# A two-layer decoder in float32 on one core: choosing when ordinary matmul units are put between Strassen units, and regrouping fifteen weight tiles

## The chip, the cores and the metric

The kernel runs on one core of one Trainium2 chip. The metric is the device time of one launch in microseconds (us), lower is better. Three timed runs of the kernel before gave 2006.13, 2009.50 and 2009.53 us, so the median is 2009.5 us.

## The reference

Two layers work on 256 tokens of width 2048, all in float32. Each layer is

```
h  = RMSNorm(x);  z = h @ w_in                      # 2048 -> 3584
A  = chunked spatial gating of gelu(z[:, :2048])
B  = windowed attention on the rest of z
x += concat(RMSNorm(A), RMSNorm(B)) @ w_out         # 2048 -> 2048
h2 = RMSNorm(x)
x += (silu(h2 @ w_gate) * (h2 @ w_up)) @ w_down     # 2048 -> 5632 -> 2048
```

Only the last line is touched by the change in the order of its work. The buffers that the change regroups are used by all the matmuls with weights.

## The kernel before, in words

**Tiles.** Weights come from HBM in tiles of 128 partitions x 1024 float32 (512 KB), each holding two 128x512 blocks. The matmuls with weights take the type float32r, and a weight tile is split into a high and a low part: `split2` (line 91) lets ScalarE copy the raw tile into `wh` (line 97, a CAST in the profile) and VectorE subtract that from the raw tile into `wl` (line 98). A product of two split operands is three matmuls (`mm3`, lines 126 to 129: high x high, high x low, low x high). An *ordinary unit* (`unit`, line 131) is one raw tile against both groups of 128 tokens: 12 matmuls of 128x512.

**Rings.** Raw tiles live in 7 buffers, `wh` in 4 and `wl` in 4, 15 tiles of 4 KB a partition together. A buffer comes free when its last reader is done: a raw buffer after the subtraction on VectorE, `wl` after the last line-128 matmul of its unit, `wh` after the last line-129 matmul. The sum `t1` of the Strassen units also takes a raw buffer. Loads are issued by SyncE (queue SP) in order, each as soon as a raw buffer is free.

**The feed-forward part.** Eleven blocks of 512 columns of w_gate and w_up are computed. Blocks 0, 1 and 2 are computed by ordinary units (`gate_up`). Blocks 3 to 10 are computed by `seven` (line 571), a Strassen scheme with seven products in place of eight for the two token groups and the two matrices. Each of its *Strassen units* (`s_unit`) is one tile against one 128-token operand: 6 matmuls. A block has two phases. In phase A there are four rounds; each loads three raw tiles, makes three further sums of tiles on VectorE (`t1`, `t2`, and `b12` in place, lines 595, 598, 601) and runs four Strassen units into the PSUM tiles m0, m1, m3, m2. A DMA on POOL's queue then adds w_gate's fourth tile onto `t2` in place (line 603), to be kept for phase B. After the rounds, one ScalarE copy and four VectorE operations on 128x512 recombine the banks (lines 609 to 616). In phase B four rounds load two raw tiles each and run three Strassen units into n0, n1, n2, and five VectorE operations and two SiLUs finish the block (lines 630 to 635).

**The order.** Two Python generators are interleaved when the program is written. `s_stream` yields after each Strassen unit and after each recombination; `std_stream` yields after each ordinary unit of `gate_up` and `down`. The loop at lines 696 to 703 says how many ordinary units come in between: 0.575 of one per Strassen unit in phase A, 0.23 in phase B and 2 at each recombination, kept in the account `owed`, at most one at a time between two Strassen units. `down` of a block can't begin until that block's activations have been transposed (`act_T`, lines 559 to 565): the stream then yields False and no ordinary unit is written. After the Strassen blocks the rest of the ordinary units follows alone (line 705). An ordinary unit in this part accumulates in the two PSUM tiles `dacc`; the next group of sums can't start before VectorE has taken both out (`xres`, line 683). A list scheduler then orders the instructions of each engine near the written order; in the trace each engine works its own list off in order.

Of the kernel before, what the change touches and what calls it, by code (L numbers as in the profile page):

```python
# [12 lines left out]
F32 = mybir.dt.float32  # L13
# [8 lines left out]
P = 128  # L22
# [13 lines left out]
NB = 512  # L36
# [8 lines left out]
    ("gu", 0), ("down", (0, 3)), ("gu", 1), ("down", (1, 4)), ("down", (5, 6)), ("gu", 2),  # L45
    ("down", (2, 7)), ("down", (8, 9)), ("down", (10,)),
)
SHARE_A = 0.575
SHARE_B = 0.23
TURN = 2  # L50
RL = 512
WARM = 12

# [12 lines left out]
def trunk(ctx, tc, x, xt, w_in, w_out, w_gate, w_up, w_down, sgu_w, sgu_g, consts,  # L66
# [15 lines left out]
        return t.bitcast(F32)  # L82

    def raw_load(src, parts=1):
        raw = wp.tile([P, 2, NB], F32, tag="raw", name="raw", bufs=7)
        n = 2 // parts
        for i in range(parts):
            nc.sync.dma_start(raw[:, i * n : (i + 1) * n, :], src[:, i * n : (i + 1) * n, :])
        return raw

    def split2(raw):
        wh = wp.tile([P, 2, NB], F32R, tag="wh", name="wh", bufs=4)
        wl = wp.tile([P, 2, NB], F32R, tag="wl", name="wl", bufs=4)
        step = 2 if clock[0] > 1 else 1
        for j in range(0, 2, step):
            src = raw[:, j : j + step, :]
            nc.scalar.copy(wh[:, j : j + step, :], src)  # L97
            nc.vector.tensor_tensor(  # L98
                wl[:, j : j + step, :], src, f(wh[:, j : j + step, :]), ALU.subtract
            )  # L100
        return wh, wl

    clock = [0]
    serial = itertools.count()
    pending = []

# [24 lines left out]
    def unit(src, acts, acc, first, last):  # L131
        raw = raw_load(src, 2 if clock[0] < 4 else 1)
        wh, wl = split2(raw)
        for j in range(2):
            act, aj = acts[j]
            for t in range(NTOK):
                ts = slice(t * P, (t + 1) * P)
                mm3(
                    acc[t], act[:, 0, aj, ts], act[:, 1, aj, ts], wh[:, j, :], wl[:, j, :],
                    first and j == 0, last and j == 1,  # L140
                )
        tick()

    def product(srcs, pairs):
# [114 lines left out]
    for lay in range(L):  # L259
# [299 lines left out]
        def act_T(b, c, sg, pairs_f=pairs_f):  # L559
            ps = pm.tile([P, 2, SEQ], F32, tag="sm", name="ps_f")  # L560
            transpose_pair([sg[t][:, 2 * c * P : (2 * c + 2) * P] for t in range(NTOK)], ps)
            pair = tp.tile([P, 2, 2, SEQ], F32R, tag="aT", name="aT")
            nc.scalar.copy(pair[:, 0], ps)
            nc.vector.tensor_tensor(pair[:, 1], ps, f(pair[:, 0]), ALU.subtract)
            pairs_f.setdefault(b, []).append(pair)

        def act_later(b, sg, act_T=act_T):
# [3 lines left out]
        def seven(b, lay=lay, pairs2=pairs2, ext2=ext2, act_later=act_later):  # L571
            bank = [pa.tile([P, NB], F32, tag="acc", name=f"m{i}") for i in range(4)]

            def s_unit(raw, m, i, op, first, last):
                wh, wl = split2(raw)
                for j in range(2):
                    ah, al = (op(2 * i + j, h) for h in range(2))
                    mm3(bank[m], ah, al, wh[:, j, :], wl[:, j, :], first and j == 0, last and j == 1)
                tick(0.5)

            def a_op(k, t):
                return lambda p, h: pairs2[p][:, h, k, t * P : (t + 1) * P]

            def e_op(n):
                return lambda p, h: ext2[p][:, h, n, :]

            kept = []
            for i in range(4):
                b11 = raw_load(w_gate[lay, b, i, 0])
                b12 = raw_load(w_up[lay, b, i, 0])  # L590
                b22 = raw_load(w_up[lay, b, i, 1])
                t1 = wp.tile([P, 2, NB], F32, tag="raw", name="t1", bufs=7)
                t2 = ap.tile([P, 2, NB], F32, tag="spt", name="t2", bufs=4)
                first, last = i == 0, i == 3
                nc.vector.tensor_tensor(t1, b11, b12, ALU.add)
                s_unit(b11, 0, i, a_op(0, 0), first, last)
                yield SHARE_A
                nc.vector.tensor_tensor(t2, t1, b22, ALU.add)
                s_unit(t1, 1, i, e_op(1), first, last)
                yield SHARE_A  # L600
                nc.vector.tensor_tensor(b12, b12, b22, ALU.add)  # L601
                s_unit(t2, 3, i, e_op(2), first, last)
                nc.gpsimd.dma_start(t2, w_gate[lay, b, i, 1], accum_op=ALU.add)  # L603
                yield SHARE_A
                s_unit(b12, 2, i, e_op(0), first, last)
                yield SHARE_A
                kept.append(t2)
            m1 = zp.tile([P, NB], F32, tag="z", name="m1")
            nc.scalar.copy(m1, bank[0])
            u1 = zp.tile([P, NB], F32, tag="z", name="u1")  # L610
            nc.vector.tensor_tensor(u1, bank[3], m1, ALU.add)
            c22 = zp.tile([P, NB], F32, tag="z", name="c22")
            c21 = zp.tile([P, NB], F32, tag="z", name="c21")
            nc.vector.tensor_tensor(c21, bank[2], u1, ALU.add)
            nc.vector.tensor_tensor(c22, bank[1], c21, ALU.add)
            nc.vector.tensor_tensor(u1, bank[1], u1, ALU.add)
            yield "turn"
            bank = [pa.tile([P, NB], F32, tag="acc", name=f"n{i}") for i in range(3)]
            for i in range(4):
                b21 = raw_load(w_gate[lay, b, i, 1])  # L620
                b22 = raw_load(w_up[lay, b, i, 1])
                first, last = i == 0, i == 3
                s_unit(b21, 0, i, a_op(1, 0), first, last)
                yield SHARE_B
                s_unit(kept[i], 1, i, a_op(1, 1), first, last)
                yield SHARE_B
                s_unit(b22, 2, i, e_op(3), first, last)
                yield SHARE_B
            sg = [m1, c21]
            for t, m in ((0, m1), (1, c21)):  # L630
                nc.vector.tensor_tensor(m, bank[t], m, ALU.add)
                nc.scalar.activation(m, m, AF.Silu, scale=rstd2[t])
            nc.vector.tensor_tensor(u1, bank[2], u1, ALU.add)
            for t, c in ((0, u1), (1, c22)):
                nc.vector.scalar_tensor_tensor(sg[t], c, nrstd2[t], sg[t], ALU.mult, ALU.mult)
            act_later(b, sg)
            yield "turn"

        seven_done = [False]

# [13 lines left out]
        def gate_up(b, even=even, act_later=act_later):  # L654
            acc = yield from even(b, w_gate)
            sg = []
            for t in range(NTOK):
                s = zp.tile([P, NB], F32, tag="z", name="sg")
                nc.scalar.activation(s, acc[t], AF.Silu, scale=rstd2[t])
                sg.append(s)  # L660
            acc = yield from even(b, w_up)
            for t in range(NTOK):
                nc.vector.scalar_tensor_tensor(
                    sg[t], acc[t], rstd2[t], sg[t], ALU.mult, ALU.mult
                )
            act_later(b, sg)

        def down(blocks, final, lay=lay, pairs_f=pairs_f, norm_block=norm_block, ss1=ss1, pairs1=pairs1):
            for n in range(ND):
                while any(len(pairs_f.get(b, [])) < 2 for b in blocks):  # L670
                    yield False
                acc = new_acc() if seven_done[0] else new_acc(pd, "dacc")
                for k, b in enumerate(blocks):
                    for c in range(2):
                        pair = pairs_f[b][c]
                        unit(
                            w_down[lay, b, n, c], [(pair, 0), (pair, 1)], acc,
                            k == 0 and c == 0, k == len(blocks) - 1 and c == 1,
                        )
                        yield True  # L680
                for t in range(NTOK):
                    xs = xres[:, t, n * NB : (n + 1) * NB]
                    nc.vector.tensor_tensor(xs, acc[t], xs, ALU.add)  # L683
                    if final and lay == L - 1:
                        nc.sync.dma_start(out[t * P : (t + 1) * P, n * NB : (n + 1) * NB], xs)
                if final and lay < L - 1:
                    norm_block(n, ss1, pairs1, lay + 1, C_G1)
# [6 lines left out]
                    yield from down(what, k == len(STD_ORDER) - 1)  # L694

        other = std_stream()
        owed = 0.0
        for said in s_stream():
            turn = said == "turn"
            owed += TURN if turn else said  # L700
            for k in range(TURN):
                if (turn or (k == 0 and owed >= 1.0)) and next(other, False):
                    owed -= 1.0
        seven_done[0] = True
        for went in other:
            if not went:
# [89 lines left out]
```

## Time and profile before

| what | value |
|---|---|
| timed runs, median | 2009.5 us |
| profiled execution, own time | 2011.28 us |
| its span, first to last instruction | 2009.6 us, so 1.7 us lie around it |
| granted TensorE clock, mean | 0.995 |
| TensorE matmuls | 8942, of which 8064 of 128x512 with weights |
| HBM traffic | 226 GB/s over the span |
| feed-forward parts | 299 to 980 us and 1300 to 1980 us of the span |

TensorE is the engine that sets the time. A matmul of 128x512 is shown as 0.39 us long, but the next one starts 0.227 us after it, so starts are compared here and not ends. VectorE operations on 128x1024 are shown as 1.22 us long and follow each other every 1.14 us; those on 128x512 are shown as 0.69 us and follow each other every 0.60 us.

### The profile page before, as it was taken

How to read it: one execution, taken by the hardware profiler on the slowest of the kernel's cores; microseconds unless marked ns; L12 is line 12 of the kernel's file. 1: busy time of each engine (PE TensorE's matmuls, PEld its weight loads, DVE VectorE, ACT ScalarE, POOL GpSimd, SP SyncE). 2: the span in 40 equal slices, each digit the busy share in tenths (PEclk: the TensorE clock that was granted, in tenths of full speed). 3: DMA queues.
4: the chain of work that ended last, by engine and by line, in shares of the span. 5: the costliest groups of instructions: out<-in, count | busy, mean ns of one | idle time of the engine just before them, and what ended most of it. 6: DMA issues, size and time to landing. Idle time of an engine off the chain costs nothing.

```text
span 2009.6 us, 24839 instructions
## 1 busy us (share of the span) xinstructions
PE 1971.9 (98%) x8942; PEld 1610.9 (80%) x8942; DVE 1664.0 (83%) x1931; ACT 1154.1 (57%) x1441; POOL 120.0 (6%) x129
## 2 busy tenths in 40 slices
PE   9999999999999999999999999999999999999999
PEld 6778887788878887788887788877888788877887
DVE  6767689989899897889866776889898998978896
ACT  6455566655655565555654655666556565555554
POOL 1211001000000000000002110000000000000000
PEclk9999999999999999999999999999999999999999
DMA  8753558787796876868655445487887878868684
GB/s 313 254 160 130 188 165 262 216 275 236 247 275 219 274 237 231 252 211 286 216 189 184 138 147 188 159 273 219 262 242 248 274 218 272 251 222 264 208 275 154
DMA packets 127772, 453.80 MB, mean 226 GB/s; under 512 B 14064, under 2 KB 16240, under 8 KB 127648
## 3 DMA queue, kind: packets, MB, share of 16 engines
q1 hardware_dynamic: 116288, 411.21, 60.1%
q0 software_dynamic: 11360, 41.00, 11.1%
q8 instruction: 70, 1.15, 0.2%
q14 instruction: 54, 0.44, 0.1%
HBM read 450.02 MB, written 4.23 MB: 226 GB/s over the span
## 4 chain that ended last, share of the span: by engine, by line
PE 83%; DVE 11%; issue 2%; DMA 2%; ACT 1%; POOL 1%; SPq 0%; DVEq 0%; POOLq 0%; ACTq 0%
PE dacc L128 11%; PE dacc L129 11%; PE dacc L127 10%; PE acc L128 8%; PE acc L129 8%; PE acc L127 7%; DVE wl L98 5%; PE m L129 4%; PE m L128 4%; PE m L127 4%; PE n L128 4%; PE n L129 4%; PE n L127 4%; DMA raw<-in_w_up_dram 1%; DVE raw L601 1%
## 5 line engine op out<-in xcount | busy, mean ns | idle before, releaser
L97 ACT CAST wh<-raw 128x1024 fp32r<-128x1024 f32 (+1 forms) x706 | 738.5, 1050 | 565.6 <-PE dacc L129 215.5
L98 DVE TENSOR_TENSOR wl<-raw,wh 128x1024 fp32r<-128x1024 f32 (+1 forms) x706 | 854.4, 1219 | 199.0 <-ACT wh L97 183.9
L97 ACT CAST wh<-t 128x1024 fp32r<-128x1024 f32 x192 | 202.3, 1054 | 186.9 <-PE dacc L129 109.7
L128 PE MATMUL dacc<-wl,aT 128*128 128x512 f32 x640 | 251.4, 393 | 8.5 <-DVE wl L98 8.5
L98 DVE TENSOR_TENSOR wl<-t,wh 128x1024 fp32r<-128x1024 f32 x192 | 233.5, 1222 | 21.5 <-ACT wh L97 16.3
L129 PE MATMUL dacc<-wh,aT 128*128 128x512 f32 x640 | 251.0, 392 | 0.0
L127 PE MATMUL dacc<-wh,aT 128*128 128x512 f32 x640 | 249.7, 392 | 0.7 <-DVE xres L683 0.7
L128 PE MATMUL acc<-wl,hT 128*128 128x512 f32 x448 | 177.0, 395 | 7.9 <-DVE wl L98 7.9
L127 PE MATMUL acc<-wh,hT 128*128 128x512 f32 x448 | 181.2, 407 | 0.8 <-ACT wh L97 0.8
L129 PE MATMUL acc<-wh,hT 128*128 128x512 f32 x448 | 177.1, 395 | 0.0
L127 PE MATMUL m<-wh,ext 128*128 128x512 f32 x384 | 153.3, 399 | 3.7 <-ACT wh L97 3.5
L128 PE MATMUL dacc<-wl,hT 128*128 128x512 f32 x384 | 150.5, 392 | 3.3 <-DVE wl L98 3.3
L128 PE MATMUL m<-wl,ext 128*128 128x512 f32 x384 | 150.6, 392 | 0.6 <-DVE wl L98 0.2
L127 PE MATMUL dacc<-wh,hT 128*128 128x512 f32 x384 | 150.7, 392 | 0.1
L129 PE MATMUL dacc<-wh,hT 128*128 128x512 f32 x384 | 150.2, 391 | 0.0
L129 PE MATMUL m<-wh,ext 128*128 128x512 f32 x384 | 150.0, 391 | 0.0
L128 PEld LDWEIGHTS dacc<-wl,aT 128*128 128x128 f32 x640 | 121.0, 189 | 36.1 <-DVE wl L98 11.1
L127 PEld LDWEIGHTS dacc<-wh,aT 128*128 128x128 f32 x640 | 120.8, 189 | 26.8 <-DVE xres L683 1.6
L129 PEld LDWEIGHTS dacc<-wh,aT 128*128 128x128 f32 x640 | 121.0, 189 | 25.0
L603 POOL DMA_DIRECT2D t<-in_w_gate_dram x64 | 54.5, 852 | 1387.2 <-DVE wl L98 754.6
L127 PE MATMUL acc<-wh,aT 128*128 128x512 f32 x320 | 126.9, 397 | 0.0
L129 PE MATMUL acc<-wh,aT 128*128 128x512 f32 x320 | 125.2, 391 | 0.0
(157 smaller groups left out, 3146.4 us busy)
## 6 DMA issues: line engine op xcount, KB each, us to landing
raw<-in_w_up_dram SPq DMA_DIRECT2D x240, 512.0 KB, 4.7
raw<-in_w_gate_dram SPq DMA_DIRECT2D x176, 512.0 KB, 4.7
raw<-in_w_down_dram SPq DMA_DIRECT2D x176, 512.0 KB, 4.6
raw<-in_w_in_dram SPq DMA_DIRECT2D x108, 512.0 KB, 4.3
raw<-in_w_out_dram SPq DMA_DIRECT2D x64, 512.0 KB, 3.3
t<-in_w_gate_dram POOLq DMA_DIRECT2D x64, 512.0 KB, 7.0
bias<-rdram POOLq DMA_DIRECT2D x8, 512.0 KB, 5.2
xr<-in_xt_dram SPq DMA_DIRECT2D x8, 256.0 KB, 5.7
```

The source lines that it names most:

```text
L97: nc.scalar.copy(wh[:, j : j + step, :], src)
L98: nc.vector.tensor_tensor(wl[:, j : j + step, :], src, f(wh[:, j : j + step, :]), ALU.subtract)
L127: nc.tensor.matmul(acc, ah, wh, start=first, stop=False)
L128: nc.tensor.matmul(acc, ah, wl, start=False, stop=False)
L129: nc.tensor.matmul(acc, al, wh, start=False, stop=last)
L601: nc.vector.tensor_tensor(b12, b12, b22, ALU.add)
L603: nc.gpsimd.dma_start(t2, w_gate[lay, b, i, 1], accum_op=ALU.add)
```

## The change

Two edits.

1. The 15 weight tiles are dealt out anew: 6 raw, 5 `wh`, 4 `wl` in place of 7, 4, 4.
2. The fixed shares are replaced by a running count. Each VectorE operation of the feed-forward part adds to `debt` (1.14 for 128x1024, 0.6 for 128x512), each matmul takes away 0.227 x 0.91 = 0.207. After every Strassen unit and recombination, ordinary units are written until the count is no longer above zero, or the stream yields False. The order inside each stream and all arithmetic stay.

```diff
-SHARE_A = 0.575
-SHARE_B = 0.23
-TURN = 2
+VEC = 1.14
+VEC_P = 0.6
+MM = 0.227
+LOAD = 0.91
...
     def raw_load(src, parts=1):
-        raw = wp.tile([P, 2, NB], F32, tag="raw", name="raw", bufs=7)
+        raw = wp.tile([P, 2, NB], F32, tag="raw", name="raw", bufs=6)
...
     def split2(raw):
-        wh = wp.tile([P, 2, NB], F32R, tag="wh", name="wh", bufs=4)
+        wh = wp.tile([P, 2, NB], F32R, tag="wh", name="wh", bufs=5)
         wl = wp.tile([P, 2, NB], F32R, tag="wl", name="wl", bufs=4)
...
+        vec(1)
         return wh, wl
...
+    debt = [0.0]
+
+    def vec(n, cost=VEC):
+        debt[0] += n * cost
+
+    def pe(n):
+        debt[0] -= n * MM * LOAD
...
     def unit(src, acts, acc, first, last):
...
+        pe(12)
         tick()
...
             def s_unit(raw, m, i, op, first, last):
...
+                pe(6)
                 tick(0.5)
...
-                t1 = wp.tile([P, 2, NB], F32, tag="raw", name="t1", bufs=7)
+                t1 = wp.tile([P, 2, NB], F32, tag="raw", name="t1", bufs=6)
...
                 nc.vector.tensor_tensor(t1, b11, b12, ALU.add)
                 s_unit(b11, 0, i, a_op(0, 0), first, last)
-                yield SHARE_A
+                vec(1)
+                yield
...
-            yield "turn"
+            vec(4, VEC_P)
+            yield
...
                 s_unit(b21, 0, i, a_op(1, 0), first, last)
-                yield SHARE_B
+                yield
...
+            vec(5, VEC_P)
             act_later(b, sg)
-            yield "turn"
+            yield
...
         other = std_stream()
-        owed = 0.0
-        for said in s_stream():
-            turn = said == "turn"
-            owed += TURN if turn else said
-            for k in range(TURN):
-                if (turn or (k == 0 and owed >= 1.0)) and next(other, False):
-                    owed -= 1.0
+        debt[0] = 0.0
+        for _ in s_stream():
+            while debt[0] > 0.0 and next(other, False):
+                pass
```

The count is also fed, with 0.6 for each VectorE operation, in `act_T` (one, and two matmuls' worth taken away), at the end of `gate_up` (two) and for each `xres` in `down`.

More of the change, by code (lines that the diff above doesn't have):

```diff
@@ L564, in act_T @@
             nc.vector.tensor_tensor(pair[:, 1], ps, f(pair[:, 0]), ALU.subtract)
+            vec(1, VEC_P)
+            pe(2)
             pairs_f.setdefault(b, []).append(pair)
@@ L596, in seven @@
                 s_unit(b11, 0, i, a_op(0, 0), first, last)
-                yield SHARE_A
+                vec(1)
+                yield
                 nc.vector.tensor_tensor(t2, t1, b22, ALU.add)
                 s_unit(t1, 1, i, e_op(1), first, last)
-                yield SHARE_A
+                vec(1)
+                yield
                 nc.vector.tensor_tensor(b12, b12, b22, ALU.add)
@@ L603, in seven @@
                 nc.gpsimd.dma_start(t2, w_gate[lay, b, i, 1], accum_op=ALU.add)
-                yield SHARE_A
+                vec(1)
+                yield
                 s_unit(b12, 2, i, e_op(0), first, last)
-                yield SHARE_A
+                yield
                 kept.append(t2)
@@ L616, in seven @@
             nc.vector.tensor_tensor(u1, bank[1], u1, ALU.add)
-            yield "turn"
+            vec(4, VEC_P)
+            yield
             bank = [pa.tile([P, NB], F32, tag="acc", name=f"n{i}") for i in range(3)]
@@ L623, in seven @@
                 s_unit(b21, 0, i, a_op(1, 0), first, last)
-                yield SHARE_B
+                yield
                 s_unit(kept[i], 1, i, a_op(1, 1), first, last)
-                yield SHARE_B
+                yield
                 s_unit(b22, 2, i, e_op(3), first, last)
-                yield SHARE_B
+                yield
             sg = [m1, c21]
@@ L635, in seven @@
                 nc.vector.scalar_tensor_tensor(sg[t], c, nrstd2[t], sg[t], ALU.mult, ALU.mult)
+            vec(5, VEC_P)
             act_later(b, sg)
-            yield "turn"
+            yield
         seven_done = [False]
@@ L665, in gate_up @@
                 )
+            vec(NTOK, VEC_P)
             act_later(b, sg)
@@ L683, in down @@
                     nc.vector.tensor_tensor(xs, acc[t], xs, ALU.add)
+                    vec(1, VEC_P)
                     if final and lay == L - 1:
```

## Prediction

> **What bounds the kernel now.** I read the page's busy shares first, then TensorE's waits, then single stretches, then the timeline.
>
> ```profile
> ## 1 busy us (share of the span) xinstructions
> PE 1971.9 (98%) x8942; PEld 1610.9 (80%) x8942; DVE 1664.0 (83%) x1931; ACT 1154.1 (57%) x1441; POOL 120.0 (6%) x129
> ```
>
> TensorE is busy nearly always, and the change adds and removes no instruction that computes. So only TensorE's stalls can be won, or new ones made. TensorE's waits name them:
>
> ```profile
> PE dacc L128 <- DVE wl L98: 11.8, 8, 1.9
> PE acc L128 <- DVE wl L98: 7.9, 5, 2.9
> PE m L127 <- ACT wh L97: 3.5, 6, 0.6
> PE n L127 <- ACT wh L97: 2.3, 2, 1.1
> ```
>
> Columns: total us, times, longest. It is always the split that is late. In the timeline I took every matmul start that came later than the 0.227 us pitch: clusters above 0.4 us sum to 49 us. Of these 3.3 are the warm-up, 1.1 the first loads, 12.3 lie in the attention parts (at 64 us 1.2, 128 us 3.8, 1088 us 3.5, 1128 us 3.9), and 32.8 in the two feed-forward parts. In layer 0 the latter are: first phase A 1.8; where the first, second and third ordinary gate_up end 2.7, 2.5 and 6.0; at 768 us 4.0. Layer 1 repeats them with 15.7 in place of 17.0. So about 45 us, 2.2%, is all that can be won.
>
> ```profile
> 384.00:408.00 24.00, 22.06 (x98) 16.96 (x98) 23.68 (x24) 13.40 (x15) 1.72 (x3) 1.00 0.88 263
> 440.50:468.10 27.60, 27.60 (x126) 22.84 (x125) 24.48 (x24) 18.38 (x19) 0.00 (x0) 1.00 0.61 190
> 468.10:523.30 55.20, 55.20 (x247) 45.48 (x246) 50.01 (x48) 31.85 (x33) 3.40 (x4) 1.00 0.92 284
> 811.00:834.00 23.00, 19.67 (x81) 14.78 (x80) 21.09 (x22) 11.84 (x14) 2.55 (x3) 0.93 0.86 247
> ```
>
> Columns: length, busy us of PE, PEld, DVE, ACT, POOL, granted clock, DMA share, GB/s. Two stretches without stalls (a phase B at 440 us, a phase A at 468 us) stand between two with. At 384 us VectorE is busy 23.7 of 24.0 us: there it is the bound. The reason is in the code: gate_up has ended, `down` waits for transposed activations, so no ordinary unit may be written for six Strassen units, and those cost VectorE more than TensorE.
>
> **Part 1, the count.** Prices: 1.14 us for a full VectorE operation, 0.6 for a half one (pitches of the trace); on TensorE 1.36 us for a Strassen unit, 2.72 for an ordinary one, 0.45 for four transposes. I tallied both programs, as built, phase by phase. Before: phase A 52 to 56 us of TensorE with VectorE at 0.89 to 0.98 of it, phase B 28 to 30 us at 0.79 to 0.87. After: phase A 57 to 62 us at 0.87 to 0.90 (the first and the seventh are 0.98 and 1.01), phase B 19 to 22 us at 0.93 to 1.00 (the seventh 0.79), with its twelve Strassen units in a row. So ordinary units move from B to A, and about six a layer to the tail behind the Strassen blocks, where VectorE has room (0.7). No DMA is added.
>
> The forecast is made of the stalls one by one. From the end of a block's last n2 unit, I add VectorE's list up to a late subtraction, and TensorE's up to the unit that needs it.
>
> - First gate_up, before: 19 full and 9 half operations, 27.1 us; TensorE gets there after 4 ordinary and 9 Strassen units and 16 transposes, 24.9. 2.2 late; the trace lost 2.7, so the tally is 0.5 low.
> - The same, after: 22 full and 8 half, 29.9; TensorE 5 and 10 units and 12 transposes, 28.6. 1.3 late, with the 0.5 it is 1.8.
> - Second, after: at the worst unit 0.1 late; I take 0.3. Before it had the order of the first (2.5 lost).
> - Third, after: the end of gate_up now falls at the end of phase A. VectorE 35 full and 7 half, 44.1; TensorE 9 and 17 units and 8 transposes, 48.5. Not late; I take 0.5 (before 6.0).
> - First phase A: load 0.98 in both; 1.8 stays.
> - New: at the end of the third Strassen block, the list has two `xres` behind five recombining operations. 5.2 us to the next subtraction against 4.08 + 0.23 until TensorE needs it, and the next `dacc` isn't free earlier: 0.8.
>
> **Part 2, the rings.** Before, ScalarE's copy for the fourth unit ahead waits for a `wh` buffer (325 us of ScalarE's waits end with a `dacc` matmul), then come 1.05 us of copy and 1.22 of subtraction. With five, the copy is done early, and the subtraction waits only for `wl`. The lead over TensorE grows by 1.05 us. The stall at 768 us is this ring: copies for three ordinary units had been made at 761.7, 763.0 and 767.1 but stand behind n1 in TensorE's list; n1's copy got its buffer at 769.6, when n0 was done. I count 0.5 there.
>
> The price is the raw ring. Here I add VectorE's work between the operation that frees a buffer and the first that reads the new load. The median in the feed-forward part falls from 10.3 to 8.0 us. Loads land 4.7 us after issue (w_gate, w_up); where a subtraction comes first, 1.15 for the copy are added. Gaps below that sum to 21 us a layer before and 28 after. Measured, TensorE lost little of the 21, since VectorE has room. The other ends: nothing at all; or a landing of 5.8 us, by which 45 becomes 79 us a layer. I take half of the 7, so 3.5 a layer, as landings near the median are the rule. In the attention and projection parts a raw tile lies ready for 13 us, so a buffer less costs nothing; if that cover were gone it would cost one load, 4.7 us.
>
> More PE instructions now signal (the `wl` release): 1892 instead of 1191. In the trace a line-129 matmul that signals is followed after 227.0 ns, one that doesn't after 227.6, so nothing; bounds 0 to 0.
>
> In attention the new rings also reorder VectorE's list. At 128 us the subtraction stands behind 8.3 us of small operations, among them two waits of 1.5 us for POOL; after the change both requests stand together and one wait is covered. At 1088 us a stretch of 6.7 us is cut to 5.3. Between 0 and 9 of the 12.3 us, I take 5, from these 1.5 twice and 1.4 plus what the slow clock adds.
>
> **A rule beside the rows.** After the stalls at 770 and 829 us, starts are 0.427 us apart seven to eight times, and the granted clock of 811 to 834 us is 0.93. About 25 such starts in the feed-forward parts cost 0.2 each, 5 of the 32.8 us, and go with their stalls. The Trainium skill (TensorE: Matmul & The Clock Gate, "HAM oscillation — how this bites in real kernels") has the clock drop only for idle gaps over about 3.4 us. By that rule stalls of 1.3 and 2.1 us would cost only themselves, and the sum would be 5 us higher, 1997; the trace disagrees.
>
> **The sum.** Feed-forward per layer after: 1.8 + 1.8 + 0.3 + 0.5 + 0.5 + 0.8 = 5.7, two layers 11.4 in place of 32.8: -21.4. Raw ring +7. Attention -5. Together -19.4. Against the profiled execution, 2011.28 - 19.4 = 1991.9, say **1992 us**; its 2009.6 span becomes 1990. It stands 1.8 above the median of the timed runs, so against that the gain is 17.5 us, 0.9%. Without the raw price and with 9 in attention: 1981.
>
> **Rivals.**
>
> - *All feed-forward stalls melt* (chance 0.08): the longer lead also takes the 11.4 us that I left, and the raw ring costs nothing. 2011.3 - 32.8 - 5 = 1973.5. For it speaks that no late split of the waits above is over 2.9 us; against it that VectorE is itself full at 384 us.
> - *The count can't reach the stalls* (0.17): while `down` yields False nothing can be placed, and the deeper `wh` ring doesn't help an engine that is full. Then only the rise of VectorE's work over TensorE's in these places counts: 7.7, 7.7 and 8.4 us become 7.1, 7.1 and 6.4. That is 3.2 a layer and 5 in attention: 2000.
> - *Phase B without ordinary units* (0.13): at 1.00 of TensorE's time the lead isn't rebuilt in B, and five recombining operations and a subtraction (4.14 us) meet a lead of four Strassen units less copy and subtraction, 5.44 - 2.27 = 3.2. 0.9 at 14 boundaries: 1992 + 13, about 2005. The stall-free B at 440 us, at 0.83, can't deny it. The Trainium skill (Perfetto Trace Analysis, "Optimization Strategy") says that a kernel whose bound changes over time may gain by interleaving its regimes; leaving B alone goes against that, and no run here shows it yet.
> - *The raw ring becomes the bound* (0.15), the case on the slower side. Place: phase A, where a round's b12 keeps its buffer to the last unit and the next b12 is issued only then. VectorE's spare time in a layer's Strassen part is 614 - 563 = 51 us by the tally. Gaps reach that at a landing of 5.3 us and 79 at 5.8. The excess of 28 a layer goes to TensorE: 56 in place of 32.8, attention -5: 2011 + 23 - 5 = 2029. For it: a quarter of the raw tiles in the feed-forward part are already read within some 2.4 us of landing; against it: VectorE waited only 9.6 us for loads in `t1`.
>
> **From this to the numbers.** The forecast has the rest, 0.47, by its unknown bounds 1981 to 2003. Range 1978 to 2012: it holds the forecast, the second and the third rival, 0.77, and the first steps of the fourth (a ring that costs little more than its spare time), 0.03. 0.2%, which is about what a measurement of this kernel can tell from no change, is 4 us: faster is below 2005.5. Faster: 0.47 + 0.08 + 0.17 + a third of the third, 0.76. Same: the rest of the third and a little of the raw ring, 0.10. Slower 0.14.
>
> **What would show it.** Right: no stall at 768 us's place; those at the second and third gate_up below 1 us; ScalarE's waits for `dacc` matmuls much shorter; phases A near 60 us and B near 20. Wrong: TensorE waiting for splits at each change from B to A (third rival); waits of ScalarE and VectorE for raw loads well above the 52 us of now (fourth); the three gate_up stalls unchanged (second).

## The result and the profile after

The changed kernel takes 2017.05 us (median, 2010.09 to 2024.29) and the kernel before 2009.19 (2005.8 to 2009.53): ratio 1.0048 [1.0033, 1.0064], slower by 0.5%. The forecast was 1992 us, range 1978 to 2012, so both the sign and the range were wrong. The profiled execution took 2019.19 us, its span is 2017.5.

The first lines of the page after:

```profile
span 2017.5 us, 25282 instructions
## 1 busy us (share of the span) xinstructions
PE 1974.9 (98%) x8942; PEld 1604.6 (80%) x8942; DVE 1663.5 (82%) x1931; ACT 1133.2 (56%) x1437; POOL 121.0 (6%) x129
```

VectorE and TensorE do the same work as before (1664.0 and 1971.9). So, as before, only the stalls differ. TensorE's waits after (total us, times, longest; lines have moved by about ten, the split's copy is now L98 and its subtraction L99):

```profile
PE dacc L138 <- DVE wl L99: 9.9, 18, 0.8
PE dacc L137 <- DVE xres L703: 9.7, 8, 2.3
PE m L138 <- DVE wl L99: 4.5, 6, 2.5
PE dacc L137 <- ACT wh L98: 2.7, 4, 1.2
```

These seem no worse than before: `acc` has all but gone from the list, and `xres` has grown from 0.7 to 9.7 us. They name the last link only. What moved is one link further back, in ScalarE's waits, first before, then after:

```profile
ACT wh L97 <- DMA raw<-in_w_down_dram: 26.1, 15, 3.2
ACT wh L97 <- DMA raw<-in_w_gate_dram: 8.0, 9, 2.5
ACT wh L97 <- DMA raw<-in_w_up_dram: 0.9, 2, 0.5
```

```profile
ACT wh L98 <- PE dacc L139: 147.6, 94, 5.7
ACT wh L98 <- DMA raw<-in_w_down_dram: 110.2, 47, 5.9
ACT wh L98 <- DMA raw<-in_w_up_dram: 57.8, 18, 7.0
ACT wh L98 <- DMA raw<-in_w_gate_dram: 42.8, 16, 5.5
ACT wh L98 <- DVE raw L617: 38.2, 25, 5.5
```

Waits for feed-forward weights rose from 35 to 211 us, with a longest of 7.0 in place of 3.2. The wait for a `wh` buffer (behind a `dacc` matmul) fell from 325 to 147.6 us. That it would fall was foreseen, but only part of this is the fifth buffer: in a run below with seven raw and five `wh` buffers (e3) it stands at 236 us. For the rest, ScalarE now waits for loads instead.

To see where the time went I divided both traces at the first Strassen matmul of each layer and at the last ordinary one of layer 0, and in each part summed what matmul starts come later than their pitch:

| part | before: us | lost | after: us | lost |
|---|---|---|---|---|
| first attention | 298.9 | 17.4 | 294.2 | 12.9 |
| feed-forward 0 | 707.9 | 21.0 | 720.1 | 32.9 |
| projection and attention 1 | 292.6 | 14.8 | 284.5 | 6.9 |
| feed-forward 1 and the end | 710.1 | 20.0 | 718.7 | 28.3 |

So the attention parts gained 12.8 us and the feed-forward parts lost 20.8, where I had forecast a gain of 14.4 (-21.4 and +7).

One stall from its cause to its end, in the changed kernel's timeline (start, length, engine, line; in brackets the idle time before it and what ended it):

```profile
1577.23 1.22 DVE L617 TENSOR_TENSOR raw<-raw 128x1024 f32<-128x1024 f32 x1
...
1578.47 6.04 SPq L89 DMA_DIRECT2D raw<-in_w_down_dram  x4
1578.53 1.05 ACT L98 CAST wh<-raw 128x1024 fp32r<-128x1024 f32 x1 [0.71 <-DVE raw L617]
...
1579.62 1.23 DVE L99 TENSOR_TENSOR wl<-raw,wh 128x1024 fp32r<-128x1024 f32 x1
...
1579.87 0.85 POOL L619 DMA_DIRECT2D t<-in_w_gate_dram  x1 [8.42 <-DVE wl L99]
...
1589.01 2.15 ACT L98 CAST wh<-raw 128x1024 fp32r<-128x1024 f32 x2 [3.71 <-DMA raw<-in_w_down_dram]
...
1590.09 1.23 DVE L99 TENSOR_TENSOR wl<-raw,wh 128x1024 fp32r<-128x1024 f32 x1 [2.37 <-ACT wh L98]
...
1595.01 1.28 DVE L703 TENSOR_TENSOR xres<-dacc,xres 128x512 f32<-128x512 f32 x2
...
1595.84 0.77 PE L137 MATMUL dacc<-wh,aT 128*128 128x512 f32 x1 [2.27 <-DVE xres L703]
...
1596.41 0.63 PE L138 MATMUL dacc<-wl,aT 128*128 128x512 f32 x1
...
1596.84 0.63 PE L139 MATMUL dacc<-wh,aT 128*128 128x512 f32 x1
```

Read it from the top. b12 of the block's last round has its sum (1577.23), its copy (1578.53) and its subtraction, which ends at 1580.84. That is the last read of its raw buffer, which a load at 1563.16 had taken. The next `w_down` load starts at 1580.87, one of the four that the second line groups. It lands at 1588.91, and ScalarE, idle for 3.71 us, copies at once. VectorE had nothing to subtract for 2.37 us. It goes on late through four recombining operations and another subtraction to the two `xres`. TensorE, which waits for their PSUM buffer, loses 2.27 us, and the cause turns up 15 us later under another name. The buffer was let go late, but the landing was slow too, 8.0 us. After 4.5 us, the median of this kernel's feed-forward loads, the tile would have been there as ScalarE finished its copy before, at 1585.3. Through all but the last 0.2 us of that landing, the DMA on POOL's queue that began at 1579.87 was in flight as well (the last section tells of these landings).

### The profile page after: what moved, and what is told of

Its sections match the earlier page's. It is cut to its first block, busy times and chain, and to the rows that moved or that the text cites. A ratio compares the mean times of both kernels' runs of the same rounds, so it can differ in the third digit from the quotient of the medians.

```text
span 2017.5 us, 25282 instructions
## 1 busy us (share of the span) xinstructions
PE 1974.9 (98%) x8942; PEld 1604.6 (80%) x8942; DVE 1663.5 (82%) x1931; ACT 1133.2 (56%) x1437; POOL 121.0 (6%) x129
## 5 line engine op out<-in xcount | busy, mean ns | idle before, releaser
L98 ACT CAST wh<-raw 128x1024 fp32r<-128x1024 f32 (+1 forms) x706 | 735.5, 1050 | 633.4 <-PE acc L139 169.5
L99 DVE TENSOR_TENSOR wl<-raw,wh 128x1024 fp32r<-128x1024 f32 (+1 forms) x706 | 852.1, 1218 | 224.2 <-ACT wh L98 71.9
L98 ACT CAST wh<-t 128x1024 fp32r<-128x1024 f32 x192 | 200.7, 1050 | 126.1 <-PE dacc L139 56.3
L99 DVE TENSOR_TENSOR wl<-t,wh 128x1024 fp32r<-128x1024 f32 x192 | 233.5, 1221 | 13.1 <-issue 3.4
L137 PE MATMUL dacc<-wh,aT 128*128 128x512 f32 x576 | 227.7, 396 | 12.4 <-DVE xres L703 9.7
L138 PE MATMUL dacc<-wl,aT 128*128 128x512 f32 x576 | 226.9, 394 | 4.1 <-DVE wl L99 3.9
L139 PE MATMUL dacc<-wh,aT 128*128 128x512 f32 x576 | 226.2, 393 | 0.0
L137 PE MATMUL acc<-wh,aT 128*128 128x512 f32 x384 | 151.5, 395 | 0.0
L139 PE MATMUL acc<-wh,aT 128*128 128x512 f32 x384 | 149.9, 390 | 0.0
L138 PE MATMUL acc<-wl,aT 128*128 128x512 f32 x384 | 149.5, 389 | 0.0
L137 PEld LDWEIGHTS dacc<-wh,aT 128*128 128x128 f32 x576 | 108.8, 189 | 40.0 <-DVE xres L703 5.1
L138 PEld LDWEIGHTS dacc<-wl,aT 128*128 128x128 f32 x576 | 108.9, 189 | 30.3 <-DVE wl L99 8.5
```

The costliest lines, as they stand in the source:

```text
L99: nc.vector.tensor_tensor(wl[:, j : j + step, :], src, f(wh[:, j : j + step, :]), ALU.subtract)
L137: nc.tensor.matmul(acc, ah, wh, start=first, stop=False)
L138: nc.tensor.matmul(acc, ah, wl, start=False, stop=False)
L139: nc.tensor.matmul(acc, al, wh, start=False, stop=last)
```

## The experiments

Theory: the sixth raw buffer less is what costs, because ScalarE takes the copies in order and waits for loads that start only when a buffer comes free; the count and the fifth `wh` gain about what was forecast. First rival: the count itself costs, by phases B without ordinary units. "a/b/c" are the raw, `wh` and `wl` rings; "zp" is a pool of small tiles of 2 KB in each partition, cut from eight to six where a ring of 4 KB tiles needs the room.

| run | placement | rings | zp | median us | ratio to before [95%] |
|---|---|---|---|---|---|
| e1_rings | shares | 6/5/4 | 8 | 2032.62 | 1.012 [1.0106, 1.0133] |
| e2_count | count | 7/4/4 | 8 | 1992.59 | 0.9921 [0.9908, 0.9934] |
| e8_count744z6 | count | 7/4/4 | 6 | 1992.23 | 0.9917 [0.9902, 0.9933] |
| e9_count844z6 | count | 8/4/4 | 6 | 1990.37 | 0.991 [0.9894, 0.9926] |
| e3_count754 | count | 7/5/4 | 6 | 1974.88 | 0.9833 [0.982, 0.9846] |
| e4_old754 | shares | 7/5/4 | 6 | 1973.75 | 0.9826 [0.9808, 0.9844] |
| e3c_count654z6 | count | 6/5/4 | 6 | 2023.7 | 1.0084 [1.0062, 1.0106] |
| e5_count554 | count | 5/5/4 | 8 | 2082.54 | 1.0377 [1.0353, 1.0402] |

**The two halves of the change.** The rings alone, in the kernel before:

```diff
-        raw = wp.tile([P, 2, NB], F32, tag="raw", name="raw", bufs=7)
+        raw = wp.tile([P, 2, NB], F32, tag="raw", name="raw", bufs=6)
...
-        wh = wp.tile([P, 2, NB], F32R, tag="wh", name="wh", bufs=4)
+        wh = wp.tile([P, 2, NB], F32R, tag="wh", name="wh", bufs=5)
...
-                t1 = wp.tile([P, 2, NB], F32, tag="raw", name="t1", bufs=7)
+                t1 = wp.tile([P, 2, NB], F32, tag="raw", name="t1", bufs=6)
```

> The old placement by fixed shares with the new rings, six raw, five high, four low. Theory 1 (the sixth raw buffer is what costs): the feed-forward parts lose as much as in the changed kernel, ScalarE waits some 200 us for raw loads where it waited 42, and the attention parts gain their 11 us, so about 2015 us, ratio 1.003. Theory 2 (the new placement is what costs: ordinary units in bunches, phase B without any): nothing is lost in the feed-forward parts and the attention parts gain, so about 1998 us, ratio 0.994, and ScalarE's waits for loads stay below 80 us.

And the count alone, the changed kernel with the rings of before (the same lines, backwards):

> The running count with the old rings, seven raw, four high, four low. Theory 1: the loads are early again, ScalarE's waits for them fall to about 50 us, and the count shows its own worth: 1995 to 2005 us, ratio about 0.996. Theory 2: the bunches cost what they cost in the changed kernel, and the attention gain is missing on top: 2020 to 2028 us, ratio about 1.008.

The rings alone cost 24 us, the count alone gains 16. The count does not cost; the rings do. They cost 18 us more under the old shares than e1's theory had expected.

**Seven raw and five `wh` together**, with the count and with the old shares, and the control for the smaller pool:

```diff
-    zp = ctx.enter_context(tc.tile_pool(name="zp", bufs=8))
+    zp = ctx.enter_context(tc.tile_pool(name="zp", bufs=6))
...
-        raw = wp.tile([P, 2, NB], F32, tag="raw", name="raw", bufs=6)
+        raw = wp.tile([P, 2, NB], F32, tag="raw", name="raw", bufs=7)
...
-                t1 = wp.tile([P, 2, NB], F32, tag="raw", name="t1", bufs=6)
+                t1 = wp.tile([P, 2, NB], F32, tag="raw", name="t1", bufs=7)
```

> The running count with seven raw, five high and four low buffers; the room comes from the pool of small tiles (6 in place of 8). Theory 1: waits for loads as before the change, the deeper high ring on top: 1985 to 1995 us, ratio 0.990. Theory 2: no gain over the changed kernel, 2012 to 2020 us.

> Control for the run with seven raw buffers: the changed kernel with the pool of small tiles cut from 8 to 6 and nothing else. By both theories within 5 us of the changed kernel, 2012 to 2022 us, if the small tiles are not what waits; what it differs by is to be taken off the run with seven.

> The old placement with seven raw, five high and four low buffers (room from the small tiles). It leaves only the fifth high buffer against the kernel before. Theory 1 (raw ring and placement add up): the attention parts gain their 12 us, the stalls at 768 us and its like go, the three gate_up stalls stay: 1984 to 1992 us, so the running count would be worth 10 to 15 us at these rings. Rival: with the deeper high ring the placement no longer matters, 1972 to 1978 us.

One raw buffer at five `wh` is worth 48.8 us (e3c less e3), 42 against the changed kernel itself. Cutting zp costs nothing in e8 against e2; e3c is 6.6 us above the changed kernel with intervals that just overlap, so the price lies between 42 and 49. Under the old shares the same buffer is worth 59 us (e1 less e4). ScalarE's waits for loads in e3:

```profile
ACT wh L98 <- DMA raw<-in_w_down_dram: 30.8, 19, 3.4
ACT wh L98 <- DMA raw<-in_w_gate_dram: 20.7, 11, 3.6
ACT wh L98 <- DMA raw<-in_w_up_dram: 12.5, 12, 2.2
```

64 us in place of 211. The same phase A (16 Strassen and 14 ordinary units) after and in e3 (length, busy us of PE, PEld, DVE, ACT, POOL, granted clock, DMA share, GB/s):

```profile
1539.60:1608.30 68.70, 65.12 (x282) 51.74 (x281) 57.09 (x57) 33.41 (x37) 3.39 (x4) 0.98 0.75 243
```

```profile
1509.10:1571.40 62.30, 62.10 (x281) 51.08 (x280) 56.34 (x56) 33.43 (x35) 3.39 (x4) 1.00 0.85 263
```

6.4 us of the loss are in this one phase. The phases B with one or two ordinary units lose at most 0.4 us each in both kernels.

e4 tells a second thing: with both rings long enough, the old shares are as good as the count (1973.75 and 1974.88). The count gains 16 us where `wh` is short (e2), about as much at six raw (2017.05 against e1's 2032.6), and nothing at 7/5/4.

**The ring's length.**

> The running count with seven, four, four and the pool of small tiles cut to 6. It differs from the run with 7, 5, 4 by the fifth high buffer alone, and from the run with 7, 4, 4 by the small tiles alone. If small tiles don't wait: 1990 to 1998 us; the fifth high buffer is then worth 16 to 22 us, 12 of it in attention. If they do: 2000 us or more.

> The running count with eight raw buffers and the old rings of four and four. The tally of gaps over the measured spread of landings falls from 33 to 24 us a layer. If waits for loads go to TensorE in proportion: 15 to 18 us under the run with 7, 4, 4 and small tiles 6. If VectorE's spare time swallows what is left from seven on: within 6 us of it.

> The changed kernel with one raw buffer less again, five, five, four. The tally of gaps over the spread of landings rises from 61 to 145 us a layer, 167 us in both. If the price of a raw buffer follows this tally: 2150 to 2190 us. If the sixth buffer was a step that is paid once: 2060 to 2080 us, as much again as from seven to six.

From five to six 59 us (against e3c) to 65, from six to seven 42 to 49 (at five `wh`), from seven to eight 2, within the intervals (at four `wh`; eight and five weren't tried). In e9 ScalarE waits 0.9 us in all for feed-forward weights (e2: 38), and yet only 2 us are gained: at seven, TensorE's lead must cover most of such waits. My tally of gaps, run again with the spread of the landings in place of their median, gives 52 to 56 us from six to seven, but 18 from seven to eight and 167 from five to six. It comes near the one price that was known when I ran it again, misses the two others, and is no law.

**Is it the hold of b12, or only the number of buffers?** In the changed kernel, a phase A round holds b11 for 12.3 us from issue to last read, b12 21.3, b22 13.2 and t1 9.2: together 56.0. Three orders of a round shorten b12's hold, at six raw; one takes t1 out of the ring.

| run | sum b12 + b22 made | order of the units | t1 in | holds: b11 + b12 + b22 + t1 | median us | ratio to before [95%] |
|---|---|---|---|---|---|---|
| the change | one unit ahead of its unit, in the third place | b11, t1, t2, b12 | ring | 56.0 | 2017.05 | 1.0048 [1.0033, 1.0064] |
| e10_early6 | right ahead of its unit, in the second place | b11, b12, t1, t2 | ring | 53.7 | 2012.77 | 1.0021 [1.0012, 1.0031] |
| e13_mid6 | one unit ahead, in the second place | b11, t1, b12, t2 | ring | 51.9 | 1988.2 | 0.9902 [0.9884, 0.9921] |
| e14_ahead6 | one unit ahead, in the first place | b11, b12, t1, t2 | ring | 56.0 | 2019.41 | 1.0051 [1.0036, 1.0066] |
| e12_t1own | as the change | as the change | own buffer | 50.1 without t1 | 1978.2 | 0.985 [0.9837, 0.9863] |

```diff
@@ e10_early6
                 nc.vector.tensor_tensor(t2, t1, b22, ALU.add)
+                nc.vector.tensor_tensor(b12, b12, b22, ALU.add)
+                s_unit(b12, 2, i, e_op(0), first, last)
+                vec(2)
+                yield
                 s_unit(t1, 1, i, e_op(1), first, last)
-                vec(1)
                 yield
-                nc.vector.tensor_tensor(b12, b12, b22, ALU.add)
                 s_unit(t2, 3, i, e_op(2), first, last)
                 nc.gpsimd.dma_start(t2, w_gate[lay, b, i, 1], accum_op=ALU.add)
-                vec(1)
-                yield
-                s_unit(b12, 2, i, e_op(0), first, last)
                 yield
@@ e12_t1own (with zp at 6, as above)
-                t1 = wp.tile([P, 2, NB], F32, tag="raw", name="t1", bufs=6)
+                t1 = wp.tile([P, 2, NB], F32, tag="t1", name="t1", bufs=1)
```

> The changed kernel with one edit: in a phase A round the sum b12 + b22 is made one unit earlier and its unit is placed second, so that b12 is let go after the second unit and not after the fourth; t1's unit becomes the third and t2's the fourth. The rings stay at six, five and four. Theory (long holds in the raw ring, and releases that come in order, cost the 49 us between six and seven raw buffers): b12's hold of 21 us falls by two units, some 7.5 us of a round of 15 us, which is half a buffer if b12's place in the ring is what the loads wait for, so about half of the 49 us comes back: 1990 us (1982 to 2000). If only the sum of the holds counts, t1's hold grows by one unit, 3.7 us, and the net is a quarter of a buffer: 2003 us. Rival (only the number of buffers counts, whoever holds them): 2017 us, within 4.

> The changed kernel with t1 in a single buffer of its own, and the raw ring at six for loads alone; two buffers of the small-tile pool make the room, as in the kernels with seven raw buffers. As much memory as seven, five and four. Theory (holds): t1 held a raw buffer for 9.2 of 15 us of a phase A round, 0.6 of a buffer, which the loads now have, so between 1975 us (as seven in the ring) and 1995 us (0.6 of the 49 us back from 2024). Rival (phase A isn't where the ring is short; the ordinary units' loads are): little comes back there, and the time stays above 2010 us.

e12 was the clear one: with t1 out, six buffers for loads alone give 45.5 of the 48.8 us back, so the shortage is in phase A's rounds, the only place where t1 exists. e10 gave only 4 us, which the rival (number alone) would have said too. Its waits showed why it decided nothing:

```profile
ACT wh L98 <- DVE raw L614: 135.6, 45, 5.9
ACT wh L98 <- DMA raw<-in_w_down_dram: 51.2, 37, 3.8
ACT wh L98 <- DMA raw<-in_w_up_dram: 26.7, 15, 3.6
ACT wh L98 <- DMA raw<-in_w_gate_dram: 24.2, 12, 3.5
```

The waits for loads were halved (211 to 102), but ScalarE now waits 135.6 us for VectorE's sum b12 + b22, which stood right ahead of its own split. So I put one unit between the sum and its use again, as in the change, but with both earlier in the round, in two ways:

```diff
@@ e13_mid6 (against the change)
                 nc.vector.tensor_tensor(t2, t1, b22, ALU.add)
+                nc.vector.tensor_tensor(b12, b12, b22, ALU.add)
                 s_unit(t1, 1, i, e_op(1), first, last)
-                vec(1)
+                vec(2)
                 yield
-                nc.vector.tensor_tensor(b12, b12, b22, ALU.add)
+                s_unit(b12, 2, i, e_op(0), first, last)
+                yield
                 s_unit(t2, 3, i, e_op(2), first, last)
                 nc.gpsimd.dma_start(t2, w_gate[lay, b, i, 1], accum_op=ALU.add)
-                vec(1)
-                yield
-                s_unit(b12, 2, i, e_op(0), first, last)
                 yield
@@ e14_ahead6 (against e10_early6)
                 s_unit(b11, 0, i, a_op(0, 0), first, last)
-                vec(1)
-                yield
                 nc.vector.tensor_tensor(t2, t1, b22, ALU.add)
                 nc.vector.tensor_tensor(b12, b12, b22, ALU.add)
-                s_unit(b12, 2, i, e_op(0), first, last)
-                vec(2)
+                vec(3)
                 yield
+                s_unit(b12, 2, i, e_op(0), first, last)
+                yield
```

> The changed kernel (rings at six, five and four), the sum b12 + b22 made in the second unit of a phase A round, as the first reordering had it, but its unit third: one unit stands between the sum and its use. Theory (b12's hold fills the ring, and the first reordering lost its gain to ScalarE's wait for the sum): that wait falls from 136 us back to some 40, ScalarE's waits for raw loads stay well below 211 us, b12 is held some 17.5 us, and the time is 2000 us (1995 to 2007). Rival (the number of buffers alone): 2017 us, within 4.

> The changed kernel (rings at six, five and four) with b12's unit second, as in the first reordering, and the sums t2 and b12 + b22 made in the first unit's slot, one unit ahead. Theory (hold): b12 is held some 14 us, the wait for the sum is gone, and the time is 1995 us (1985 to 2003). Rival (VectorE's work of a round then bunches in the first slot, three sums of about 1.1 us and the low parts of one tile in some 3.8 us, and the low parts come late): 2012 us or more, with ScalarE and TensorE waiting for VectorE. Rival (the number of buffers alone): 2017 us.

e13 gains 29 us with no byte of memory more, so the number of buffers alone is refuted. Its waits:

```profile
ACT wh L98 <- DMA raw<-in_w_down_dram: 82.2, 50, 3.7
ACT wh L98 <- DMA raw<-in_w_up_dram: 47.8, 22, 5.0
ACT wh L98 <- DMA raw<-in_w_gate_dram: 39.9, 17, 4.4
...
ACT wh L98 <- DVE raw L614: 15.3, 12, 3.7
```

The wait for the sum is down to 15.3 us. The waits for loads fell less than I had expected (170 us in all), but the longest from 7.0 to 5.0. That many short waits are covered by the lead and a few long ones aren't would fit this; it is not shown. e14 gains nothing, as the rival of bunched sums had it: b12 is held 18.3 us in place of the 14 expected, t1 13.6, and TensorE waits at a Strassen unit for its copy 18.1 us in 14 times (1.2 in 2 times in the changed kernel). But ScalarE waits only 13.0 us for the sum there, so it is not VectorE that makes these copies late, as that rival had supposed. ScalarE works in order. Eight of the 14 (7.6 us) come right behind copies out of PSUM, for which it had stood idle 6.1 to 6.3 us until TensorE's own matmuls were done; four (7.9 us) behind a wait of 4.1 to 5.0 us for a load, and two (2.6 us) behind a wait for a `wh` buffer.

The sums of ScalarE's waits do not price these orders: e13 and e14 wait alike for loads (170 and 173 us) and for the sum (15 and 13), and differ by 31 us; e10 waits less for loads, 102 us, and is slower than e13. The three orders also charge the count at other places. Each phase keeps its number of ordinary units, but inside a phase A some of them follow other Strassen units, and no run separates this share.

My reason in e10's expectation, that releases come in order, fell: in the stretch above, each load takes the buffer that has just been let go, 0.03 us after its last read, and passes the older b12, which is still held. So the sum of the holds may be what counts, and the four kernels with t1 in the ring do stand in its order: 51.9, 53.7, 56.0 and 56.0 for 1988, 2013, 2017 and 2019 us. The holds contain waits of their own, and four points are few, so this ranks and does not price.

**Do the two remedies add up?**

> The count with seven raw, five high and four low buffers and the order of the first edit (b12's unit second in its round). Theory: the ring is nearly long enough at seven, ScalarE's waits for raw loads fall from the 64 us of the same kernel without the edit, and the time falls by what matmul starts still lose in phase A, at most 3 us: 1972 us (1969 to 1976). Rival (the earlier sum puts a VectorE sum ahead of the unit's low parts and costs a stall each round): 1980 us or more.

> The count, rings of seven, five and four, and the order that brought six raw buffers to 1988 us (the sum b12 + b22 in the second unit's place, its unit third). Theory (the hold costs only while the ring is short): most of the 1974.9 us kernel's 14 us of matmul starts lost in the feed-forward stand at the first gate_up and at two phases A of layer 1; 2 to 6 us of them go: 1971 us (1968 to 1975). Rival (the order is worth its 29 us by itself): below 1960 us.

> The count, t1 in a buffer of its own, six raw buffers for loads alone, and the same order of a phase A round. Theory: 19 us of matmul starts are lost in the feed-forward without the order (1978 us); a shorter hold of b12 takes some half of them: 1970 us (1967 to 1976). Rival (the order is worth its 29 us by itself): below 1960 us.

| run | built of | median us | ratio to before [95%] |
|---|---|---|---|
| e11_early754 | count, 7/5/4, e10's order | 1987.71 | 0.9894 [0.9879, 0.9909] |
| e15_mid754 | count, 7/5/4, e13's order | 1973.33 | 0.9822 [0.9808, 0.9835] |
| e16_midt1own | count, t1 in its own buffer, e13's order | 1971.8 | 0.9811 [0.9797, 0.9824] |

They don't: the 29 us of e13's order shrink to 1.6 at seven raw and 6.4 with t1 outside. It is one cost, and the ring is nearly free of it there. e10's order costs 13 us at seven (the rival of e11): its wait for the sum, 162 us there, is a cost of its own. e16 is 1.9% below the kernel before, 2.2% below the changed one, and can't be told from e4 and e15.

Not every run came out as expected. Beside e1, e2 was 2 us and e3 10 us below the range of its theory, e3c 2 and e5 2.5 above theirs, and e13 7 below. e10 lay between its theory and its rival. In e4, e11 and e14 it was a rival's time that came.

## Why the prediction was wrong

**The step that failed is the raw ring term**: "I take half of the 7, so 3.5 a layer, as landings near the median are the rule", +7 in the sum. It measured 42 to 49 us. That is shown; how the term came to be so small is my reading of its working, in three points.

- *The median for the spread.* In the kernel before, feed-forward landings run from 3.3 (one in ten) to 6.5 us (nine in ten) around 4.7. At 4.7 my tally gave 21 and 28 us a layer; over the spread it gives 35 and 61, 26 a layer more, 52 in both. A gap that a median load just fits is missed by half of all loads. This is argued and not shown, as the same tally misses the other two lengths. And the spread is not even over the part: in phase A, where the ring is short, the median landing is 5.2 us, in phase B 4.2.
- *Halving.* I halved it because TensorE had lost little of the 21 before. But of the lengths tried, seven is the shortest at which it lost little; what is covered there says nothing of six.
- *The end of the range.* The upper end (45 to 79 a layer at 5.8) was written down: 68 in both layers, more than what came. I gave it to the fourth rival, not to the forecast.

**The count and the fifth `wh`** (-21.4): right in kind, mis-sized to the safe side. At seven raw the feed-forward parts of e3 are 28.8 us shorter than before. Clusters above 0.4 us leave 6.6 there in place of the forecast 11.4, all of it at the first gate_up of each layer, which I had at 1.8 and which measured 3.2 and 3.4. The stalls of the first phase A, at the second and third gate_up and at 768 us, and the 0.8 that I had added at the end of the third block, are not there in e3. What I had not seen is that the fifth `wh` is enough by itself: the shares with 7/5/4 (e4) have the feed-forward 27.0 us shorter, the count with four `wh` (e2) 14.8.

**Attention** (-5): measured -12.8, beyond my upper bound of 9. The parts shrink by 12.7 in e1 too, with the old shares, so it comes with the fifth `wh` and not with the count; the clusters at 128, 1088 and 1128 us are gone.

Sum: 7.4 better in the stalls and 7.8 in attention, 42.6 worse in the ring (49.6 by the spans of the feed-forward parts): 27.4 above the forecast, as the span shows (2017.5 against 1990).

**The rivals.** The fourth is what happened, in the place that it named, phase A, though not by the step that it gave ("the next b12 is issued only then"): loads pass a b12 that is still held, as the timeline shows. It had the feed-forward stalls grow by 23 us, and these parts grew by 20.8. Its time, 2029, is 10 above the profiled execution (2019.2), mostly for the 7.8 that attention gave beyond its 5. Its deciding point failed: a mean landing over 5.3 us was needed, and the mean stayed at 4.9: late loads cost one by one, as the stall in the timeline shows, and the mean does not tell of them. Against it I had set VectorE's short waits for loads; they stayed short (5.7 us after, L609), as ScalarE stands ahead of VectorE and takes the waits. I looked at the wrong engine.

The third rival did not come about: phases B with one or two ordinary units lose at most 0.4 us, so leaving B alone cost nothing. By the Trainium skill (Perfetto Trace Analysis, "Optimization Strategy"), a more even mix of the regimes might have gained; e4 keeps the old, more even mix and e3 the uneven one, and they agree within their intervals. The second rival is refuted by e2, where the count alone reached the stalls. The first, all of them melting at 1973.5, is nearly e3 and e4.

**The clock.** The stall of the timeline above, 2.27 us long, is followed by starts 0.427 us apart (1596.41, 1596.84) in place of 0.227. In the trace the granted clock stands at 0.5 from 1595.6 on, for 3.41 us. The feed-forward parts after have four such stretches with 27 such starts, those before three with 19 (the prediction had about 25), and those of e3 have no such start. So the stalls' surcharge, 27 times 0.2 or about 5 us, goes with them, as the prediction had it. Not every stall brings one: at 415 us TensorE is idle for 2.49 us, its longest wait for a split, and no stretch at 0.5 follows. That stalls of 2.3 us and less can bring one disagrees again with the Trainium skill (TensorE: Matmul & The Clock Gate, "HAM oscillation — how this bites in real kernels"), which wants an idle gap over 3.4 us for it.

**What stays open.** How the 29 us of e13 split between shorter holds, the earlier sum and the places of the ordinary units; how much of the ring's price is the slow landing beside POOL's DMA; and the 6.6 us between e3c and the changed kernel.

## What to carry to other kernels

Do not price a buffer less in a prefetch ring by a median landing. Look at the spread of the landings and at how long each tile holds its place in the tightest phase, and then try the length, as no tally here gave the price at all lengths: this ring cost 42 to 65 us for a buffer below seven and 2 above. Look for the wait at the engine that touches the load first, for the engine that stalls in the end names another cause. Before adding buffers, try an order that lets go of them sooner: making one sum and its unit a place earlier gave back 29 of the 42 to 49 us without memory (e13). But measure each order: making the sum right ahead of its use merely moved the wait to VectorE (e10), and a third order gained nothing (e14).

## What the runs showed of the hardware

- A load of 512 KB does not land in a fixed time, and in the changed kernel the largest difference goes with the DMA on POOL's queue that adds w_gate's fourth tile onto `t2`, issued in phase A alone (its number, its size and its median landing in us):

```profile
t<-in_w_gate_dram POOLq DMA_DIRECT2D x64, 512.0 KB, 6.9
```

- Of the 592 feed-forward loads, the 372 issued while none of these is in flight land after 4.2 us in the median, and none takes over 6.5 us. The 220 issued while one is in flight land after 5.8 us, and 62 of them take over 6.5. The kernel before shows the same, 4.3 and 5.8 us.
- Other raw loads issued in the 4 us before make a smaller difference: 3.2 us with none, 4.2 with one, 4.6 with two while no such DMA is in flight; 5.7, 5.8 and 6.4 us while one is. The load issued at 1580.87 in the timeline, with two others before it and such a DMA in flight, took 8.0 us. No run takes that DMA out, so what it costs is read off the landings and not shown by a run.
